# An encoder block in float32: the residual added by accumulating transfers, the token scale in the gate, and the last weight splits at set points

## The chip, the cores and the metric

The kernel runs on one core of a Trainium2 chip. The metric is the device time of one execution in microseconds (us). Engines are called as in the profile: PE (TensorE), DVE (VectorE), ACT (ScalarE), POOL (GpSimd), SP (SyncE); SP, ACT and POOL also issue DMA transfers, each from a queue of its own.

## The reference

One layer of a bidirectional encoder on a sequence of 512 tokens with 2048 features; the attention half is cut to a line.

```python
def reference(x, ...):
    h = rmsnorm(x, norm_attn)
    # input projection, two groups of attention heads, output projection, residual
    x = x + concatenate([ya, yb]) @ w_out
    h = rmsnorm(x, norm_ffn)
    x = x + (silu(h @ w_gate) * (h @ w_up)) @ w_down      # 2048 -> 5632 -> 2048
    return rmsnorm(x, norm_final)                         # y * rsqrt(mean(y*y) + eps) * gain
```

## The kernel before

**Splits.** Every product is made in near-float32 precision from three matmuls (`mm3`, L184 to L186): each operand is split into `hi`, a rounded copy that ACT casts, and `lo`, the rest, which DVE subtracts. So each piece of weight costs a DMA into a staging place (`st`, three of them), a cast on ACT and a subtraction on DVE.

**Stages.** Input projection and attention (to about 715 us), output projection (to 870), 44 units of gate and up (`unit_gu`, to 1750), and the down projection. Gate, up and most of down use a Strassen-like scheme with seven products ("11", "s3", "s2", "12", "s1", "22", "s4") of sums of weight quarters: `make` loads the four quarters (L583), adds (L593 to L603) and splits them (L612 on ACT, L613 on DVE), three products ahead of their use. `unit_gu` ends in Silu of the gate and its product with up, and `keep_combos` stores the sums and splits of the activations in `combos`.

**Down projection.** `unit_first` does the first two blocks of the inner dimension plainly and leaves the result in `acc[u, l]`, for four blocks `u` of 512 output features; each is a place of 128x1024 called `y`, `sums`, `raw` or `w` in the profile. Then come chunks 0 to 4, each with units u = 0 to 3: "(4,1)" is chunk 4, unit 1. A unit of chunks 0 to 3 has 168 matmuls of 128x256, one of chunk 4 has 126. After each product, DVE adds the bank to `acc` (`add`, L790, and L810 at the start of chunks 1 to 3); ACT copies some banks first (L806, L814). The activations' operands come by POOL's 1792 KB loads (L747), four around each start of a chunk. `unit_last` does the last four blocks plainly: 16 banks, one for each token tile t and block g, of 12 matmuls of 128x512.

**Last pieces.** `unit_last` needs eight pieces of weight of 128x1024, split by `fetch` (L119 load, L120 cast, L121 subtraction), and four tiles of activations, split by `act_tile` (L726 to L728). Before, `prepare_last` asks for the four tiles, the final gains (L896) and two pieces in unit (4,3) after its fourth product; the other six come when `unit_last` starts.

**Residual and final norm.** The activations lack the token scale `r2` (the factor of the second RMSNorm), so `add_x1` loads the residual (L843) and forms `y * r2 + x1` with two DVE operations of 128x256 (L847): for t = 0, 1 after each unit of chunk 4, for t = 2, 3 in `unit_last`. `to_rest` (L872) adds the last bank times `r2`. `finish` squares with a sum (ACT, L907), multiplies by the gain in place (DVE, L908), adds up (L910), and after the fourth block scales (L916 on ACT, L918 on DVE) and stores (L919).

**Order.** PE's instructions run in the order in which the units are written. For the other engines a list scheduler sets the order when the program is built; each engine and each DMA queue then works strictly in its order and waits on semaphores.

Of the kernel before, what the change touches and what calls it, by code (L numbers as in the profile page):

```python
# [10 lines left out]
F32 = mybir.dt.float32  # L11
F32R = mybir.dt.float32r
# [33 lines left out]
def encoder_block(ctx: ExitStack, tc: tile.TileContext, io):  # L46
# [34 lines left out]
    def w_tile():  # L81
        return work.tile([P, 512], F32, name="wk")
# [549 lines left out]
    def unit_gu(f):  # L632
        apart = f == 0
        al, be, gm = bank(), bank(), bank()
        de = bank() if apart else al
        into = {"11": al, "s3": gm, "s2": de, "12": be, "s1": de, "22": gm, "s4": de}
        first, second = slice(0, 256), slice(256, 512)
        a, b, g = w_tile(), w_tile(), w_tile()
        s1, u2, q7, c11 = a[:, first], a[:, second], b[:, first], b[:, second]
        if f % 2 == 0:  # L640
            four["raw"] = pools["mk"].tile([P, 1024], F32, name="raw").rearrange("p (a q) -> p a q", a=4)
        raw = four["raw"]
        out = (raw[:, 1], raw[:, 0]) if f % 2 == 0 else (raw[:, 2], raw[:, 3])
# [12 lines left out]
        def after(i):  # L656
            if i == 0:
                act.copy(s1, al[:, first])
            elif i == 1:
                act.copy(q7, gm[:, first])  # L660
            elif i == 2 and apart:
                dve.tensor_add(u2, de[:, first], s1)
                dve.tensor_add(q7, q7, s1)
            elif i == 2:
                act.copy(u2, al[:, first])  # L665
            elif i == 3:
                dve.tensor_add(c11, be[:, first], s1)
            elif i == 4:
                dve.tensor_add(g[:, second], de[:, first], q7)
            elif i == 5:  # L670
                dve.tensor_add(g[:, first], gm[:, first], u2)
                dve.tensor_mul(g, g, pools["rb2"])
# [45 lines left out]


    acts, acc, ops = {}, {}, {}  # L720
    nr2 = const.tile([P, NT], F32, name="nr2")

    def act_tile(f, a=None):
        if f not in acts:
# [24 lines left out]
    def unit_first():  # L749

        places_for_acc()
        load_operands(0)
        dve.tensor_scalar_mul(nr2, r2, -1.0)
        for u in range(DN):
            wh, wl = batch()
            if u == 3:
                limit[0] = len(UNITS) * 7
                make_to(NF * 7 + 2)
            b = [bank() for _ in range(NT)]
            for f in range(2):  # L760
                ws = slice(f * 512, (f + 1) * 512)
                for t in range(NT):
                    mm3(b[t], acts[f][:, t * P:(t + 1) * P], acts[f][:, 512 + t * P:512 + (t + 1) * P],
                        wh[:, ws], wl[:, ws], start=f == 0, stop=f == 1)
                yield
            for t in range(NT):
                o = acc[u, t // 2][:, (t % 2) * 512:(t % 2 + 1) * 512]
                act.copy(o[:, :256], b[t][:, :256])
                act.activation(o[:, 256:], b[t][:, 256:], AF.Copy, scale=-1.0)

    def unit_dn(c, u):
        pairs = CHUNKS[c]
# [13 lines left out]
        def flat(x):  # L786
            return x.rearrange("p (t q) -> p t q", t=2)

        def add(h, l, x):
            dve.tensor_add(r[h, l], flat(x), r[h, l])  # L790

        def product(i, some):
            n = PRODUCTS[i]
# [37 lines left out]
        for i in range(7):  # L831
            product(i, pairs[3:] if apart and i < 4 else pairs)
            after(i)
            if i0 == len(UNITS) - 1 and i == 3:
                prepare_last()
            yield
        if c == len(CHUNKS) - 1:
            for t in range(2):
                add_x1(t, u)

    def add_x1(t, u):
        x1 = w_tile()
        nc.sync.dma_start(x1, x1_kept[t, u])  # L843
        y = rest[t, u] = acc[u, t // 2][:, (t % 2) * 512:(t % 2 + 1) * 512]
        for h, r in enumerate((r2, nr2)):
            s = slice(h * 256, (h + 1) * 256)
            dve.scalar_tensor_tensor(y[:, s], y[:, s], r[:, t:t + 1], x1[:, s], op0=OP.mult, op1=OP.add)  # L847

    late = []

    def late_tile():

        n = len(late)
        if n % 3 == 0:
            late_tile.last = pools["xa"].tile([P, 7, 512], F32R, name=f"cp{(0, 1, 5, 2, 3)[n // 3]}")
        late.append(late_tile.last[:, 2 * (n % 3):2 * (n % 3) + 2].rearrange("p a q -> p (a q)"))
        return late[-1]

    def last_pair(i):
        if 2 <= i < 5:  # L860
            return wsh.tile([P, 1024], F32R, name="hi"), wsl.tile([P, 1024], F32R, name="lo")
        return late_tile(), late_tile()

    def prepare_last():
        for f in range(NF - CF, NF):
            act_tile(f, late_tile())
        load_gfin()
        fetch()
        fetch()

    def to_rest(t, g, b):
        dve.scalar_tensor_tensor(rest[t, g], b, r2[:, t:t + 1], rest[t, g], op0=OP.mult, op1=OP.add)  # L872

    def unit_last():
        w = [batch() for _ in range(8)]
        for t in range(NT):
            for g in range(4):
                b = bank()
                for f in range(CF):
                    a, (wh, wl) = acts[NF - CF + f], w[g * 2 + f // 2]  # L880
                    ws = slice((f % 2) * 512, (f % 2 + 1) * 512)
                    mm3(b, a[:, t * P:(t + 1) * P], a[:, 512 + t * P:512 + (t + 1) * P],
                        wh[:, ws], wl[:, ws], start=f == 0, stop=f == CF - 1)
                yield
                if t < 2:
                    add_x1(2 + t, g)
                to_rest(t, g, b)
                finish(t, g)

    gfin = []  # L890

    def load_gfin():
        gains = pools["mx"].tile([P, 7, 512], F32, name="w0")
        for j in range(2):
            t = gains[:, 2 * j:2 * j + 2].rearrange("p a q -> p (a q)")
# [5 lines left out]
    so_far = {}  # L901

    def finish(t, g):
        y = rest[t, g]
        jk = w_tile()
        col = ssq3[:, t * 4 + g:t * 4 + g + 1]
        act.activation(jk, y, AF.Square, accum_out=col)  # L907
        dve.tensor_mul(y, y, gfin[g // 2][:, (g % 2) * 512:(g % 2 + 1) * 512])  # L908
        v = small(1)
        dve.scalar_tensor_tensor(v, col, 1.0 / D, so_far.get(t, epsc), op0=OP.mult, op1=OP.add)  # L910
        so_far[t] = v
        if g == 3:
            r = rsqrt(v, 1)
            for c in range(4):
                if c % 2:
                    act.activation(rest[t, c], rest[t, c], AF.Copy, scale=r)  # L916
                else:
                    dve.tensor_scalar_mul(rest[t, c], rest[t, c], r)  # L918
                nc.sync.dma_start(io["out"][t * P:(t + 1) * P, c * 512:(c + 1) * 512], rest[t, c])  # L919


    side = []
# [131 lines left out]
```

## Time and profile before

| | |
|---|---|
| median of 3 runs | 2224.97 us (2224.67 to 2231.49) |
| profiled execution, own time | 2224.93 us |
| its span | 2223.2 us, granted PE clock 0.995 |
| busy: PE, DVE, ACT, POOL | 2187.6, 1661.5, 1000.2, 10.4 us |
| start of chunk 4; of `unit_last`; last matmul | 2101.48; 2160.84; 2212.49 us |

Times in the profile count from the start of the span. A row of a timeline is start, duration, engine, line, operation, output<-inputs and shape; what stands in brackets is the engine's idle time before it and who ended it. Durations of neighbours overlap a little, so the time that an operation takes in a full queue is read from start to start.

### The profile page before, as it was taken

The page shows a single profiled execution, that of the slowest core. Times are in us where ns is not written, and L with a number is a line of the kernel's source. Part 1 is how long each engine was busy: PE and PEld are TensorE (multiplying, and loading weights), DVE is VectorE, ACT ScalarE, POOL GpSimd, SP SyncE. Part 2 cuts the span into 40 slices and gives each one's busy share as a digit, 9 for nine tenths or more (in the row PEclk, how much of TensorE's full clock was granted, in tenths as well). Part 3 has the DMA queues.
Part 4 walks back from the last instruction along what each step waited for, and adds up shares of the span by engine and source line. Part 5 has one row for each costly group of instructions (what it writes and reads, how often), then busy time and mean ns, then how long its engine had stood idle before and what let it go on. Part 6 is the DMA issues. An engine that isn't in the chain of part 4 may idle for free. (4 is left out here: it accounts for less than half of the span.)

```text
span 2223.2 us, 37891 instructions
## 1 busy us (share of the span) xinstructions
PE 2187.6 (98%) x15754; PEld 2058.0 (93%) x15754; DVE 1661.5 (75%) x2373; ACT 1000.2 (45%) x1486; POOL 10.4 (0%) x23
## 2 busy tenths in 40 slices
PE   9999999999999999999999999999999999999997
PEld 8888888888888888999999999999999999999995
DVE  5655555676787447788888888888887498898897
ACT  6333333545555334444454444544444543343443
POOL 0000000000000000000000000000000000000000
PEclk9999999999999999999999999999999999999999
DMA  8222222222222453344454444544444746446344
GB/s 302 82 80 76 79 83 76 74 71 76 67 76 86 155 180 101 124 139 153 146 178 144 133 163 148 170 147 131 170 147 155 280 162 232 156 181 243 113 133 137
DMA packets 86908, 308.59 MB, mean 139 GB/s; under 512 B 10032, under 2 KB 11952, under 8 KB 84304
## 3 DMA queue, kind: packets, MB, share of 16 engines
q1 hardware_dynamic: 81696, 267.11, 36.8%
q0 software_dynamic: 2736, 34.87, 3.8%
q10 hardware_dynamic: 2304, 4.20, 0.5%
q8 instruction: 123, 2.02, 0.4%
q14 instruction: 49, 0.40, 0.1%
HBM read 261.31 MB, written 44.83 MB: 138 GB/s over the span
## 5 line engine op out<-in xcount | busy, mean ns | idle before, releaser
L612 ACT CAST hi<-m 128x1024 fp32r<-128x1024 f32 (+1 forms) x208 | 215.1, 1038 | 251.4 <-PE bank L185 124.4
L184 PE MATMUL bank<-cp,hi 128*128 128x256 f32 x1116 | 314.1, 281 | 0.1
L185 PE MATMUL bank<-cp,hi 128*128 128x256 f32 x1116 | 311.9, 280 | 0.0
L186 PE MATMUL bank<-cp,lo 128*128 128x256 f32 x1116 | 311.8, 279 | 0.0
L613 DVE TENSOR_TENSOR lo<-m,hi 128x1024 fp32r<-128x1024 f32 (+1 forms) x208 | 249.5, 1201 | 60.4 <-ACT hi L612 60.2
L121 DVE TENSOR_TENSOR lo<-st,hi 128x1024 fp32r<-128x1024 f32 (+1 forms) x136 | 165.0, 1214 | 142.6 <-ACT hi L120 138.9
L120 ACT CAST hi<-st 128x1024 fp32r<-128x1024 f32 (+1 forms) x136 | 141.7, 1042 | 194.9 <-PE bank L185 75.3
L185 PE MATMUL bank<-lo,cp 128*128 128x256 f32 (+1 forms) x738 | 209.0, 283 | 4.3 <-DVE lo L613 2.8
L184 PEld LDWEIGHTS bank<-cp,hi 128*128 128x128 f32 x1116 | 210.8, 189 | 0.5 <-ACT wk L665 0.3
L185 PEld LDWEIGHTS bank<-cp,hi 128*128 128x128 f32 x1116 | 210.3, 188 | 0.0
L186 PEld LDWEIGHTS bank<-cp,lo 128*128 128x128 f32 x1116 | 210.2, 188 | 0.0
L184 PE MATMUL bank<-hi,cp 128*128 128x256 f32 (+1 forms) x738 | 208.8, 283 | 0.7 <-DVE sums L790 0.7
L186 PE MATMUL bank<-hi,cp 128*128 128x256 f32 (+1 forms) x738 | 208.8, 283 | 0.0
L184 PE MATMUL bank<-xt,hi 128*128 128x512 f32 x512 | 206.3, 403 | 0.0
L184 PE MATMUL bank<-cp,m 128*128 128x256 f32 x732 | 205.4, 281 | 0.0
L185 PE MATMUL bank<-cp,m 128*128 128x256 f32 x732 | 204.2, 279 | 0.0
L186 PE MATMUL bank<-cp,m 128*128 128x256 f32 x732 | 204.2, 279 | 0.0
L186 PE MATMUL bank<-xt,lo 128*128 128x512 f32 x512 | 200.4, 391 | 0.0
L185 PE MATMUL bank<-xt,hi 128*128 128x512 f32 x512 | 199.9, 390 | 0.0
L612 ACT CAST m<-m 128x1024 fp32r<-128x1024 f32 (+1 forms) x112 | 116.8, 1043 | 144.2 <-PE bank L185 87.9
L613 DVE TENSOR_TENSOR m<-m,m 128x1024 fp32r<-128x1024 f32 (+1 forms) x112 | 135.3, 1208 | 39.1 <-ACT m L612 38.8
L185 PE MATMUL bank<-lo,xt 128*128 128x256 f32 x512 | 144.9, 283 | 0.7 <-DVE lo L121 0.6
(270 smaller groups left out, 5909.5 us busy)
## 6 DMA issues: line engine op xcount, KB each, us to landing
st<-w SPq DMA_DIRECT2D x199, 512.0 KB, 3.7
m<-w SPq DMA_DIRECT2D x180, 512.0 KB, 4.4
cp<-combos POOLq DMA_DIRECT2D x17, 1792.0 KB, 17.2
combos<-y SPq DMA_DIRECT2D x57, 512.0 KB, 4.5
combos<-y SPq DMA_DIRECT2D x19, 256.0 KB, 5.3
m<-w SPq DMA_DIRECT2D x12, 384.0 KB, 3.4
at<-x SPq DMA_DIRECT2D x8, 512.0 KB, 8.9
wk<-x SPq DMA_DIRECT2D x16, 256.0 KB, 5.3
```

The lines of the kernel that those rows point to most:

```text
L120: act.copy(hi[:, s], st[:, s])
L121: dve.tensor_sub(lo[:, s], st[:, s], hi[:, s].bitcast(F32))
L184: pe.matmul(out, lh, rh, start=start, stop=False, **kw)
L185: pe.matmul(out, lh, rl, start=False, stop=False, **kw)
L186: pe.matmul(out, ll, rh, start=False, stop=stop, **kw)
L612: act.copy(hi[:, :n], w[name])
L613: dve.tensor_sub(lo[:, :n], w[name], hi[:, :n].bitcast(F32))
```

## The change

The edit has six parts: the gate's factor is multiplied once more by the token scale after Silu (new L674); `unit_first` copies whole banks; the additions to `acc` are written as additions and subtractions (L790, L788); `add_x1` becomes two POOL transfers of 512 KB for each u that add the residual into `acc` in memory (L841), in chunk 2 after the second product; `prepare_last` spreads the last splits over chunks 3 and 4, with new places for them; the multiplication of the final norm writes to another place, and ACT issues half of the stores. Lines after L674 shift: L847 has gone, L872 is L875, L908 L911, L910 L913, L918 L924, L919 L922 on ACT and L925 on SP.

```diff
@@ unit_gu, after(i) @@
                 act.activation(g, g, AF.Silu, scale=-1.0)
+                dve.tensor_mul(g, g, pools["rb2"])
                 dve.tensor_mul(out[0], c11, g[:, first])
@@ unit_first @@
-                o = acc[u, t // 2][:, (t % 2) * 512:(t % 2 + 1) * 512]
-                act.copy(o[:, :256], b[t][:, :256])
-                act.activation(o[:, 256:], b[t][:, 256:], AF.Copy, scale=-1.0)
+                act.copy(acc[u, t // 2][:, (t % 2) * 512:(t % 2 + 1) * 512], b[t])
@@ unit_dn @@
         def add(h, l, x):
-            dve.tensor_add(r[h, l], flat(x), r[h, l])
+            if h == 1:
+                dve.tensor_add(r[h, l], r[h, l], flat(x))
+            else:
+                dve.tensor_sub(r[h, l], r[h, l], flat(x))
...
-            if i0 == len(UNITS) - 1 and i == 3:
-                prepare_last()
+            if c == 2 and i == 1:
+                add_x1((u + 2) % DN)
+            prepare_last(c, u, i)
             yield
-        if c == len(CHUNKS) - 1:
-            for t in range(2):
-                add_x1(t, u)
-
-    def add_x1(t, u):
-        x1 = w_tile()
-        nc.sync.dma_start(x1, x1_kept[t, u])
-        y = rest[t, u] = acc[u, t // 2][:, (t % 2) * 512:(t % 2 + 1) * 512]
-        for h, r in enumerate((r2, nr2)):
-            s = slice(h * 256, (h + 1) * 256)
-            dve.scalar_tensor_tensor(y[:, s], y[:, s], r[:, t:t + 1], x1[:, s], op0=OP.mult, op1=OP.add)
+
+    def add_x1(u):
+        for l in range(2):
+            pool.dma_start(acc[u, l].rearrange("p (t q) -> p t q", t=2),
+                           x1_kept[2 * l:2 * l + 2, u].rearrange("t p q -> p t q"), accum_op=OP.add)
...
-    def prepare_last():
-        for f in range(NF - CF, NF):
-            act_tile(f, late_tile())
-        load_gfin()
-        fetch()
-        fetch()
+    def prepare_last(c, u, i):
+        if (c, u, i) in ((3, 3, 3), (4, 1, 1), (4, 1, 4), (4, 3, 3), (4, 3, 4)):
+            fetch()
+        if (c, u, i) == (4, 2, 4):
+            load_gfin()
+        if c == 4 and u == 0 and i in (1, 4):
+            for f in range(2):
+                act_tile(NF - CF + f + (i == 4) * 2, take())
 
     def to_rest(t, g, b):
-        dve.scalar_tensor_tensor(rest[t, g], b, r2[:, t:t + 1], rest[t, g], op0=OP.mult, op1=OP.add)
+        y = rest[t, g] = acc[g, t // 2][:, (t % 2) * 512:(t % 2 + 1) * 512]
+        dve.tensor_add(y, b, y)
@@ unit_last @@
-                if t < 2:
-                    add_x1(2 + t, g)
                 to_rest(t, g, b)
                 finish(t, g)
@@ finish @@
         act.activation(jk, y, AF.Square, accum_out=col)
-        dve.tensor_mul(y, y, gfin[g // 2][:, (g % 2) * 512:(g % 2 + 1) * 512])
+        z = done_y[t, g] = rest[t - 1, g] if t else spare[g] if g < 3 else w_tile()
+        dve.tensor_mul(z, y, gfin[g // 2][:, (g % 2) * 512:(g % 2 + 1) * 512])
...
                 if c % 2:
-                    act.activation(rest[t, c], rest[t, c], AF.Copy, scale=r)
+                    act.activation(z, z, AF.Copy, scale=r)
+                    act.dma_start(o, z)
                 else:
-                    dve.tensor_scalar_mul(rest[t, c], rest[t, c], r)
-                nc.sync.dma_start(io["out"][t * P:(t + 1) * P, c * 512:(c + 1) * 512], rest[t, c])
+                    dve.tensor_scalar_mul(z, z, r)
+                    nc.sync.dma_start(o, z)
```

The scheduler gives the engines the following orders. First SP's queue around chunk 4, before: the quarters of units (4,1) to (4,3) (L583, `m` and `st`), the residual's loads (L843), the activation tiles (L726) and the last pieces of weight (L119).

```order
382 L896 DMA w_22754<-gfin 128x1024 x2
383 L583 DMA m_22270<-w 128x768
384 L583 DMA st<-w 128x768
385 L843 DMA wk<-x_kept 128x512 x2
386 L583 DMA m_22268<-w 128x768
387 L583 DMA m_22264<-w 128x768
388 L583 DMA m_22459<-w 128x768
389 L583 DMA st<-w 128x768
390 L843 DMA wk<-x_kept 128x512 x2
...
394 L726 DMA st<-acts_kept 128x512 x3
...
397 L119 DMA st<-w 128x1024 x2
...
399 L119 DMA st<-w 128x1024 x6
```

The same queue after:

```order
378 L119 DMA st<-w 128x1024
...
383 L726 DMA st<-acts_kept 128x512
...
385 L726 DMA st<-acts_kept 128x512
386 L583 DMA m_22320<-w 128x768
387 L726 DMA st<-acts_kept 128x512 x2
388 L583 DMA m_22318<-w 128x768
389 L583 DMA m_22314<-w 128x768
390 L583 DMA st<-w 128x768
391 L119 DMA st<-w 128x1024 x2
392 L583 DMA m_22508<-w 128x768
...
395 L583 DMA st<-w 128x768
396 L119 DMA st<-w 128x1024 x5
```

The activation tiles and three of the eight pieces now stand among the quarters of chunk 4, and the residual's loads are gone. DVE's queue between units (4,2) and (4,3), before, with the residual's operations (L847):

```order
2097 L790 TENSOR_TENSOR raw<-wk,raw 128x2x256
2098 L613 TENSOR_TENSOR m_22532<-m_22264,m_22531 128x768
2099 L790 TENSOR_TENSOR raw<-bank,raw 128x2x256
2100 L613 TENSOR_TENSOR lo<-m_22453,hi 128x768
2101 L790 TENSOR_TENSOR raw<-wk,raw 128x2x256
2102 L790 TENSOR_TENSOR w_18264<-bank,w_18264 128x2x256
2103 L596 TENSOR_TENSOR st<-st,m_22457 128x768
2104 L613 TENSOR_TENSOR lo<-st,hi 128x768
2105 L790 TENSOR_TENSOR raw<-bank,raw 128x2x256
2106 L598 TENSOR_TENSOR m_22453<-st,m_22453 128x768
2107 L847 SCALAR_TENSOR_TENSOR raw<-raw,r_99,wk 128x256
2108 L790 TENSOR_TENSOR w_18264<-bank,w_18264 128x2x256
```

And after; the last row is the `lo` of product s2 of unit (4,3):

```order
2144 L790 TENSOR_TENSOR w_18307<-w_18307,bank 128x2x256
2145 L613 TENSOR_TENSOR lo<-st,hi 128x768
2146 L790 TENSOR_TENSOR raw<-raw,bank 128x2x256
2147 L596 TENSOR_TENSOR st<-st,m_22508 128x768
2148 L121 TENSOR_TENSOR m_22784<-st,m_22783 128x1024
2149 L598 TENSOR_TENSOR m_22504<-st,m_22504 128x768
2150 L788 TENSOR_TENSOR w_18307<-w_18307,bank 128x2x256
2151 L613 TENSOR_TENSOR m_22689<-m_22510,m_22688 128x768
2152 L121 TENSOR_TENSOR m_22809<-st,cp_22445 128x1024
2153 L613 TENSOR_TENSOR lo<-m_22504,hi 128x768
```

Two subtractions L121 for `unit_last` now stand among the additions and splits of chunk 4; two more (2116 and 2125) stand further ahead. POOL's queue around chunk 2, after; before, it has only the L747:

```order
16 L747 DMA cp_19616<-combos 128x3584
17 L841 DMA raw<-x_kept 128x2x512
18 L841 DMA w_18307<-x_kept 128x2x512
19 L747 DMA cp_20287<-combos 128x3584
20 L747 DMA cp_20517<-combos 128x3584
21 L747 DMA w_20519<-combos 128x3584
22 L747 DMA cp_20521<-combos 128x3584
23 L841 DMA w_18307<-x_kept 128x2x512 x2
24 L841 DMA y<-x_kept 128x2x512 x3
25 L841 DMA sums<-x_kept 128x2x512
```

Two accumulating transfers stand ahead of the loads at the start of chunk 2, and six behind them.

More of the change, by code (lines that the diff above doesn't have):

```diff
@@ L720, in encoder_block @@
     acts, acc, ops = {}, {}, {}
-    nr2 = const.tile([P, NT], F32, name="nr2")
     def act_tile(f, a=None):
@@ L752, in unit_first @@
         load_operands(0)
-        dve.tensor_scalar_mul(nr2, r2, -1.0)
         for u in range(DN):
@@ L849, in encoder_block @@
[L849 to L857, printed above, removed]
-    def last_pair(i):
-        if 2 <= i < 5:
-            return wsh.tile([P, 1024], F32R, name="hi"), wsl.tile([P, 1024], F32R, name="lo")
-        return late_tile(), late_tile()
-    def prepare_last():
-        for f in range(NF - CF, NF):
-            act_tile(f, late_tile())
-        load_gfin()
-        fetch()
-        fetch()
+    def add_x1(u):
+        for l in range(2):
+            pool.dma_start(acc[u, l].rearrange("p (t q) -> p t q", t=2),
+                           x1_kept[2 * l:2 * l + 2, u].rearrange("t p q -> p t q"), accum_op=OP.add)
@@ new lines, in encoder_block, with take @@
+    free, left, spare, gains = [], [0, 1, 5], [], []
+    def last_pair(i):
+        if i == 0:
+            return place(7, F32R), place(9, F32R)
+        if i < 3:
+            return take(), take()
+        if i == 3:
+            return place(at[0] % 6, F32R), place((at[0] + 1) % 6, F32R)
+        if i == 4:
+            return take(), place((at[0] + 2) % 6, F32R)
+        return wsh.tile([P, 1024], F32R, name="hi"), wsl.tile([P, 1024], F32R, name="lo")
+    def take():
+        if not free:
+            w = pools["xa"].tile([P, 7, 512], F32R, name=f"cp{left.pop(0)}")
+            free.extend(w[:, 2 * j:2 * j + 2].rearrange("p a q -> p (a q)") for j in range(3))
+        return free.pop(0)
@@ L892, in load_gfin @@
     def load_gfin():
-        gains = pools["mx"].tile([P, 7, 512], F32, name="w0")
+        gains.append(pools["mx"].tile([P, 7, 512], F32, name="w0"))
+        spare.extend(gains[0][:, j] for j in range(4, 7))
         for j in range(2):
-            t = gains[:, 2 * j:2 * j + 2].rearrange("p a q -> p (a q)")
+            t = gains[0][:, 2 * j:2 * j + 2].rearrange("p a q -> p (a q)")
             nc.sync.dma_start(t, io["gfin"][:, j * 1024:(j + 1) * 1024].to_broadcast([P, 1024]))
@@ L899, in encoder_block @@
     ssq3 = const.tile([P, 16], F32, name="ssq3")
-    so_far = {}
+    so_far, done_y = {}, {}
     def finish(t, g):
@@ L914, in finish @@
             for c in range(4):
+                z = done_y[t, c]
+                o = io["out"][t * P:(t + 1) * P, c * 512:(c + 1) * 512]
                 if c % 2:
-                    act.activation(rest[t, c], rest[t, c], AF.Copy, scale=r)
-                else:
-                    dve.tensor_scalar_mul(rest[t, c], rest[t, c], r)
-                nc.sync.dma_start(io["out"][t * P:(t + 1) * P, c * 512:(c + 1) * 512], rest[t, c])
+                    act.activation(z, z, AF.Copy, scale=r)
+                    act.dma_start(o, z)
+                else:
+                    dve.tensor_scalar_mul(z, z, r)
+                    nc.sync.dma_start(o, z)
     side = []
```

## The prediction

> **What bounds the kernel now.** I read the page's first part, then busy time by stages, then the chain of PE's waits, then the timelines of the stages in which PE waits.
>
> The first row is the span; the second says that PE is busy for 98% of it, so only places where PE stops can give time back.
>
> ```profile
> span 2223.2 us, 37891 instructions
> PE 2187.6 (98%) x15754; PEld 2058.0 (93%) x15754; DVE 1661.5 (75%) x2373; ACT 1000.2 (45%) x1486; POOL 10.4 (0%) x23
> ```
>
> Busy time by stage: the first row lies in the gate-and-up stage, the second is the middle of the down projection (chunk 2), the third 46 us of chunk 4, the last the 16 banks of `unit_last`.
>
> ```profile
> core 0: us, PE busy (x) PEld busy (x) DVE busy (x) ACT busy (x) POOL busy (x), PEclk, DMA share, GB/s
> 1000.00:1600.00 600.00, 599.95 (x5054) 599.44 (x5053) 509.59 (x616) 290.20 (x390) 0.00 (x0) 1.00 0.47 153
> 1947.00:2028.00 81.00, 78.15 (x671) 77.98 (x671) 69.98 (x75) 32.15 (x36) 2.11 (x4) 0.98 0.53 194
> 2104.42:2150.35 45.93, 45.93 (x392) 45.93 (x391) 45.81 (x67) 21.52 (x29) 0.00 (x0) 1.00 0.37 116
> 2160.84:2212.89 52.05, 46.82 (x194) 35.34 (x192) 43.56 (x107) 21.57 (x43) 0.00 (x0) 1.00 0.47 157
> ```
>
> Gate-and-up: PE never waits, DVE is at 85%. Chunk 4: PE never waits, but DVE has 0.12 us to spare in 46. `unit_last`: PE loses over 5 us even by this count. PE's waits from 1770 us on (engine, line, releaser: total, times, longest):
>
> ```profile
> PE bank L184 <- DVE wk L810: 8.5, 3, 2.8
> PE bank L185 <- DVE cp L121: 3.1, 4, 0.8
> PE bank L185 <- DVE lo L613: 2.8, 1, 2.8
> PE bank L185 <- DVE lo L121: 1.4, 2, 1.3
> ```
>
> L810 and L613 are the starts of chunks 1 to 3 and of chunk 0. The L121 rows are `unit_last`, waiting for the splits of its own weights. How much that stage loses in all (first and last matmul, and three between; 192 matmuls):
>
> ```profile
> 2160.84 0.40 PE L184 MATMUL bank<-cp,cp 128*128 128x512 f32 x1
> ...
> 2167.38 0.50 PE L185 MATMUL bank<-lo,cp 128*128 128x512 f32 x1 [1.29 <-DVE lo L121]
> ...
> 2178.35 0.50 PE L185 MATMUL bank<-cp,cp 128*128 128x512 f32 x1 [0.76 <-DVE cp L121]
> 2178.69 0.40 PE L186 MATMUL bank<-cp,cp 128*128 128x512 f32 x1
> ...
> 2212.49 0.39 PE L186 MATMUL bank<-cp,cp 128*128 128x512 f32 x1
> ```
>
> From 2178.69 to 2212.49 lie 147 steps without a wait, 0.230 us each. The 44 steps before them take 17.85 us instead of 44 x 0.230 = 10.12: `unit_last` loses 7.7 us, all in its first 18.
>
> **The change, part by part.**
>
> (1) *Set points for the last splits.* Gain: if every half that `unit_last` needs early is there, the 7.7 us go but for about 0.1 at its first matmul: -7.6. In the new order only three L121 stand between DVE's last chunk-4 additions and the first L872, and their pieces are the last three of eight, used 5 us or more later at 0.230 us a matmul. I take -7.6; if half of the waits return, -3.8.
>
> Cost: the splits go into chunk 4, where DVE is full. I count DVE's queue between two fixed points. It starts with the addition of `wk` in unit (4,0), which waits for ACT's copy L806 of the bank that PE has just closed, so DVE cannot be ahead there:
>
> ```profile
> 2104.42 0.69 DVE L790 TENSOR_TENSOR y<-wk,y 128x512 f32<-128x512 f32 x1 [0.70 <-ACT wk L806]
> ...
> 2132.24 0.95 DVE L613 TENSOR_TENSOR m<-m,m 128x768 fp32r<-128x768 f32 x1
> 2133.10 0.48 DVE L847 SCALAR_TENSOR_TENSOR y<-y,r,wk 128x256 f32<-128x256 f32 x1
> 2133.50 0.48 DVE L847 SCALAR_TENSOR_TENSOR y<-y,nr,wk 128x256 f32<-128x256 f32 x1
> ...
> 2136.50 0.69 DVE L790 TENSOR_TENSOR w<-bank,w 128x512 f32<-128x512 f32 x1
> 2137.10 0.95 DVE L613 TENSOR_TENSOR lo<-m,hi 128x768 fp32r<-128x768 f32 x1
> ...
> 2166.10 2.36 DVE L121 TENSOR_TENSOR lo<-st,hi 128x1024 fp32r<-128x1024 f32 x2
> 2168.38 0.48 DVE L847 SCALAR_TENSOR_TENSOR y<-y,r,wk 128x256 f32<-128x256 f32 x1
> ```
>
> From start to start: 0.866 for a 128x768 operation, 0.40 for an L847, 0.60 for a 128x512 one, 1.14 for an L121 (2.28 for two). It ends with the `lo` of product s2 of unit (4,3), which PE needs at 2150.3 (chunk 4 starts at 2101.5; three units of 126 matmuls at 0.1177 us, two products of 18). Before, 67 operations stand there: 31 x 0.866 + 24 x 0.60 + 12 x 0.40 = 46.0 us, which is the 45.93 of the window, so the count is sound. After, the 12 L847 are gone and one 128x768, three L728 and four L121 have come: 32 x 0.866 + 24 x 0.60 + 3 x 0.60 + 4 x 1.14 = 48.5 us. DVE is at that `lo` 2.6 us late without a single wait of its own, and PE stops for that long.
>
> DVE will also wait. Each split stands behind its load and ACT's cast, in one queue with the additions and the `lo` that PE needs. What these take (the first row is a load's landing around chunk 4; the second the cast, as it was in `unit_last`):
>
> ```profile
> st<-w SPq DMA_DIRECT2D x5, 512.0 KB, 4.2
> 2162.10 1.05 ACT L120 CAST cp<-st 128x1024 fp32r<-128x1024 f32 x1 [2.23 <-DMA st<-w]
> ```
>
> Walking SP's, ACT's and DVE's new queues with these durations, I get PE waits of about 0.2 us at s2 of (4,1), 1.2 at s4 of (4,1), where a fetch's cast stands ahead of L612 on ACT, and 1.1 each at s2 of (4,2) and of (4,3), where fetches wait for one of the three `st` places: 3.6 to 3.8 in all. A landing 1 us later at two of these places, as the 2.23 us idle above shows that ACT does wait for them, makes it 5.8. Ends: +2.6 and +6; I take +3.8, nearest to the walk.
>
> (2) *add_x1 as accumulating DMAs.* Removed: 32 L847, of which the 12 above are in the count of (1); the rest stood in `unit_last` beside the waits and are in the 7.7. Their 16 loads leave SP's queue, four 256 KB loads of `acts_kept` come earlier. Added: 8 POOL transfers of 512 KB. No accumulating transfer is in the trace; the nearest rows:
>
> ```profile
> st<-w SPq DMA_DIRECT2D x199, 512.0 KB, 3.7
> cp<-combos POOLq DMA_DIRECT2D x17, 1792.0 KB, 17.2
> 1934.54 0.53 POOL L747 DMA_DIRECT2D cp<-combos  x1 [80.52 <-PE bank L186]
> ...
> 1937.19 0.54 POOL L747 DMA_DIRECT2D cp<-combos  x1 [0.59 <-issue]
> ```
>
> So 3.7 to 17.2 us each. The first two are queued ahead of the four loads of 1934.5 and wait only for unit (1,2)'s last addition, one unit (168 x 0.1177 = 19.8 us) before that, so they end in time; the next two are issued at about 1938 into the burst of these loads (2 x 0.5 MB on 7.3). Each is needed two units, 40 us, after the place where it is issued. Cost 0; were (2)'s 1 MB in the burst to hold up weights by their share of it, 17.2 x 1/7.3 = 2.4 us. I take 0.
>
> (3) *Gate factor.* 44 more 128x512 multiplications, as L672:
>
> ```profile
> L613 DVE TENSOR_TENSOR lo<-m,hi 128x1024 fp32r<-128x1024 f32 x91 | 111.1, 1221 | 35.9 <-ACT hi L612 35.8
> L672 DVE TENSOR_TENSOR wk<-wk,rb 128x512 f32<-128x512 f32 x30 | 20.5, 683 | 0.0
> ```
>
> That is 0.60 from start to start, 44 x 0.60 = 26 us of DVE in a stage of 880, 85% to 88%. The cover is the first row: DVE waits 35.8 us in 30 units for ACT's casts, having run ahead of PE by as much as the buffers let it; 0.6 of 1.2 us per unit goes. Worked out over the stage, every `lo` is written at least 6 us before PE takes it. Cost 0; if the cover were gone, 26 us.
>
> (4) *unit_first's copies, additions turned round.* 32 half copies become 16; the wait there is a load's. The operation at the chunks' starts (L810, 3 x 2.8 us) keeps its place and its wait. 0, at most -0.4.
>
> (5) *Final norm.* After the last matmul:
>
> ```profile
> 2212.92 0.75 DVE L872 SCALAR_TENSOR_TENSOR w<-bank,r,w 128x512 f32<-128x512 f32 x1 [0.23 <-PE bank L186]
> 2213.76 0.63 ACT L907 ACTIVATE wk<-w 128x512 f32<-128x512 f32 x1 [1.87 <-DVE w L872]
> ...
> 2214.51 0.69 DVE L908 TENSOR_TENSOR w<-w,w 128x512 f32<-128x512 f32 x1 [0.85 <-ACT wk L907]
> 2215.12 0.15 DVE L910 SCALAR_TENSOR_TENSOR sm<-ssq,sm 128x1 f32<-128x1 f32 x1
> ...
> 2217.72 0.71 ACT L916 ACTIVATE w<-w,sm 128x512 f32<-128x512 f32 x1
> 2218.03 0.38 SPq L919 DMA_DIRECT2D out<-sums  x1
> 2218.51 0.90 SPq L919 DMA_DIRECT2D out<-w  x2
> ```
>
> L908 waits for the Square because both use one place. With a place of its own it runs beside it, and L910 can follow the Square at 2214.5 instead of 2215.12: -0.55 to -0.6. Two of the four last transfers are issued by ACT; SP's last pair takes 0.90 in a row, so about -0.2 at the end, or 0 if ACT's issue delays its second scaling by as much. I take -0.7. The Trainium skill ("DMA: Bandwidth & Descriptors", Rules for kernel authors) says that spreading transfers over the issuing queues brings no bandwidth and only saves the sequencer's issue time. By that rule alone this part is -0.2 and no more; the row agrees, since 0.90 for two is issue.
>
> **Sum.** The profiled execution took 2224.93 us (span 2223.2 and 1.7 around it), 0.04 under the median of 2224.97. -7.6 + 3.8 + 0 + 0 - 0.7 = -4.5, so 2220.4; I add 0.4, because in (1) one late landing costs 1 us and an early one wins nothing: 2220.8.
>
> **The rivals.**
>
> *Chunk 4 hides its splits.* Then 2224.9 - 7.6 - 0.7 = 2216.6. For it: chunk 2's row has DVE at 86%, so work may be pulled ahead of chunk 4. Against it: the new order already has one split there, and the count starts at an addition that PE's pace holds back.
>
> *The stall only moves.* Chunk 4's landings are late by 2 us each, five fetches and four activation tiles behind three `st` places, and PE loses 7 there: 2224.9 - 7.6 + 7 - 0.7 = 2223.6, and up to 2225.5 if 2 us of waits stay in `unit_last`. For it: DVE has no spare time to catch up.
>
> *Slower: the accumulating transfers hold the queue.* Place: start of chunk 2. POOL's queue has the first two ahead of the load of chunk 2's fourth pair, which PE needs after four early products, 4 x 18 x 0.1177 = 8.5 us after 1934.5. They have the 20 us from unit (1,2)'s end. If they take over 14 us each and loads wait for them, PE waits for the rest. [...] It makes the kernel slower by the bound below from 15.5 us each on (2 x 15.5 - 20 = 11). Against it: the 1792 KB load takes 17.2 us, four of them together, and 512 KB 3.7. [...]
>
> **Chances.** About 0.3% (6.7 us) is what a measurement of this kernel can tell from no change: faster is under 2218.3, slower over 2231.6. The forecast (DVE late in chunk 4, 2218 to 2223) 0.70; hidden 0.14; moved 0.10; slower 0.06. Faster: all of the hidden case and a little of the forecast, 0.16. Same: 0.78. The range is 2216.6 (hidden) to 2225.5 (moved), which leaves out the slower rival and a few hundredths at each end.
>
> **What would show it.** Right: no PE wait on L121 after the start of `unit_last`, about 44 us from its first to its last matmul; in chunk 4 PE waits of 3 to 5 us, released by DVE's `lo` L613 or additions, with L121 or ACT's L120 just ahead of them; gate-and-up without PE waits and DVE at 88%; the three L810 waits unchanged; the Square and the multiplication side by side. Wrong: PE waits on `cp<-combos` or weights in chunks 2 and 3, a POOL issue far above 0.53, waits in gate-and-up, or chunk 4 without waits.

## The result, and the profile after

The changed kernel takes 2242.97 us (median of 4 runs, 2242.88 to 2248.13), the kernel before beside it 2225.23 us: ratio 1.008, 95% interval 1.0064 to 1.0096. It is slower, by some 18 us (0.8%), where 2220.8 us and no change that a measurement can tell were forecast. Here and below, a ratio is estimated from all runs of both kernels, so it can differ by up to 0.1% from the quotient of the medians.

The page of the changed kernel begins:

```profile
span 2241.3 us, 37925 instructions
PE 2202.1 (98%) x15754; PEld 2071.1 (92%) x15754; DVE 1680.4 (75%) x2384; ACT 999.0 (45%) x1470; POOL 20.1 (1%) x31
```

PE has as many instructions as before and is busy 14.5 us longer, so part of the loss is not in waits at all. The stages, each measured from its first to its last matmul in the two timelines (differences in us, span against span):

| stage | before | after | difference |
|---|---|---|---|
| until gate-and-up begins | 863.2 | 862.7 | -0.5 |
| gate-and-up | 887.4 | 902.3 | +14.9 |
| `unit_first` | 21.9 | 21.9 | 0 |
| chunks 0 to 4 | 388.3 | 400.0 | +11.7 |
| `unit_last` | 51.7 | 44.4 | -7.3 |
| after the last matmul starts | 10.7 | 10.0 | -0.7 |
| sum | 2223.2 | 2241.3 | +18.1 |

The last part of the program does what the prediction said. Busy time in `unit_last` (PE is the first pair of numbers), and the tail:

```profile
2186.96:2231.70 44.74, 44.74 (x194) 35.91 (x192) 31.10 (x81) 15.83 (x37) 0.00 (x0) 1.00 0.21 71
```

```profile
2231.76 0.69 DVE L875 TENSOR_TENSOR w<-bank,w 128x512 f32<-128x512 f32 x1 [1.17 <-PE bank L186]
2232.48 0.63 ACT L909 ACTIVATE wk<-w 128x512 f32<-128x512 f32 x1 [2.08 <-DVE w L875]
2232.48 0.69 DVE L911 TENSOR_TENSOR w<-w,w 128x512 f32<-128x512 f32 x1
...
2233.24 0.16 DVE L913 SCALAR_TENSOR_TENSOR sm<-ssq,sm 128x1 f32<-128x1 f32 x1
...
2236.58 0.34 ACTq L922 DMA_DIRECT2D out<-w  x1
```

PE never stops in `unit_last`; the Square and the multiplication start at the same time, and the sum follows them. PE's waits in chunk 4:

```profile
PE bank L184 <- DVE sums L790: 1.5, 1, 1.5
PE bank L185 <- DVE lo L613: 0.9, 2, 0.5
PE bank L185 <- DVE m L613: 0.6, 1, 0.6
```

With the restart after each, these stops take 4.1 us. The longest stands at product s4 of (4,1); ahead of it ACT waits with a last piece's cast for its load, and the cast L612 that the chunk needs stands behind:

```profile
2147.97 1.05 ACT L120 CAST cp<-st 128x1024 fp32r<-128x1024 f32 x1 [2.69 <-DMA st<-w]
2148.93 1.57 ACT L612 CAST hi<-m 128x768 fp32r<-128x768 f32 x2
```

Two places where nothing was expected show new things: gate-and-up, and chunk 2. In gate-and-up, a stretch of 600 us held 5054 matmuls before; now:

```profile
1000.00:1600.00 600.00, 596.61 (x4962) 594.42 (x4962) 518.59 (x633) 284.74 (x382) 0.00 (x0) 1.00 0.45 150
```

PE is idle for 3.4 us, but 92 matmuls are missing, which is 11 us: the matmuls themselves are slower, at a granted clock of 1.00 in both. From start to start, leaving out stops, a step takes 0.1197 us instead of 0.1186. Over 44 x 168 = 7392 steps that is 8.2 us of the stage's 14.9. The rest is waits, the named ones all of one kind:

```profile
PE bank L184 <- DVE wk L669: 3.3, 6, 1.7
```

The longest of them, in the timelines of ACT, DVE and PE:

```profile
1534.15 0.62 ACT L626 CAST y<-sums 128x512 fp32r<-128x512 f32 x1 [3.41 <-DMA combos<-y]
1534.67 1.04 ACT L612 CAST hi<-st 128x1024 fp32r<-128x1024 f32 x1
```

```profile
1534.80 0.69 DVE L627 TENSOR_TENSOR y<-sums,y 128x512 fp32r<-128x512 f32 x1 [3.07 <-ACT y L626]
...
1536.88 1.21 DVE L613 TENSOR_TENSOR lo<-st,hi 128x1024 fp32r<-128x1024 f32 x1
1538.13 1.23 DVE L593 TENSOR_TENSOR st<-m,st 128x1024 f32<-128x1024 f32 x1
1539.27 0.41 DVE L669 TENSOR_TENSOR wk<-bank,wk 128x256 f32<-128x256 f32 x1
```

```profile
1539.74 0.39 PE L184 MATMUL bank<-cp,m 128*128 128x256 f32 x1 [1.66 <-DVE wk L669]
```

Read upward: PE's product s4 adds to the bank in which s1 stands, and may not begin before DVE has read it (L669). L669 stands in DVE's queue behind splits, these behind ACT's casts, and ACT stands 3.4 us at L626, the fourth split of `keep_combos`, because its place `y` is one of three and the first store from them has not landed.

The kernel before has this wait too (2.2 us on average, in each of the 19 units in which `keep_combos` makes its splits), but there it does not reach PE. The same unit before:

```profile
1520.92 0.62 ACT L626 CAST y<-sums 128x512 fp32r<-128x512 f32 x1 [2.16 <-DMA combos<-y]
1527.66 0.42 DVE L669 TENSOR_TENSOR wk<-bank,wk 128x256 f32<-128x256 f32 x1
1528.70 0.28 PE L184 MATMUL bank<-cp,m 128*128 128x256 f32 x1
```

L669 ends at 1528.08 and s4 begins at 1528.70, without a wait: 0.62 us to spare. Over the 19 units the margin was 0.5 to 0.9 us. The new multiplication takes 0.60 us of the same queue, and in the changed kernel L669 ends after PE has come to s4 in 15 of the 19 units, by up to 1.8 us.

In the chunks, PE's step went from 0.11646 to 0.11783 us (0.00137 x 3192 = 4.4 us), chunk 4 adds 4.1 us of stops, and unit (2,1) has two new ones, of 2.0 and 1.1 us (one of 0.9 us in unit (1,1) has gone):

```profile
1985.10 0.38 PE L185 MATMUL bank<-lo,cp 128*128 128x256 f32 x1 [1.84 <-DVE lo L613]
1997.52 0.36 PE L184 MATMUL bank<-hi,cp 128*128 128x256 f32 x1 [0.88 <-DVE sums L790]
```

Ahead of the first, DVE waits for a weight (the second row is its load on SP's queue):

```profile
1982.09 1.23 DVE L593 TENSOR_TENSOR st<-m,st 128x1024 f32<-128x1024 f32 x1 [5.44 <-DMA m<-w]
1970.28 0.33 SPq L583 DMA_DIRECT2D m<-w  x1
```

This weight was asked for at 1970.3 and landed 11.7 us later, where the median of such loads is 4.4 us. POOL's queue shows what was under way: the four loads of 1792 KB, and an accumulating transfer behind them.

```profile
1934.46 1.25 POOL L841 DMA_DIRECT2D raw<-x_kept  x1 [62.58 <-DVE raw L790]
1940.49 1.20 POOL L841 DMA_DIRECT2D w<-x_kept  x1 [4.79 <-issue]
1952.80 1.25 POOL L747 DMA_DIRECT2D cp<-combos  x2 [11.11 <-PE bank L186]
...
1960.93 1.22 POOL L841 DMA_DIRECT2D w<-x_kept  x1 [5.17 <-issue]
```

The transfer of 1960.9 landed after 21.2 us; the other seven, outside the burst, after 5.6 to 9.4 us. Start and landing show one thing more: each accumulating transfer that stands next behind another in POOL's queue was issued 0.3 us after that one had landed, so the queue stood still that long. Why it waits is not shown. The first two took 15.4 us in this way, and the loads were issued 2.9 us after the second had landed.

### The profile page after: what moved, and what is told of

The parts are those of the page before. It is cut to its first block, busy times and chain, and to the rows that moved or that the text cites. A ratio compares the mean times of both kernels' runs of the same rounds, so it can differ in the third digit from the quotient of the medians.

```text
span 2241.3 us, 37925 instructions
## 1 busy us (share of the span) xinstructions
PE 2202.1 (98%) x15754; PEld 2071.1 (92%) x15754; DVE 1680.4 (75%) x2384; ACT 999.0 (45%) x1470; POOL 20.1 (1%) x31
## 5 line engine op out<-in xcount | busy, mean ns | idle before, releaser
L612 ACT CAST hi<-m 128x1024 fp32r<-128x1024 f32 (+1 forms) x208 | 214.4, 1036 | 254.6 <-PE bank L185 98.2
L185 PE MATMUL bank<-cp,hi 128*128 128x256 f32 x1116 | 316.3, 283 | 0.0
L121 DVE TENSOR_TENSOR lo<-st,hi 128x1024 fp32r<-128x1024 f32 (+1 forms) x136 | 165.1, 1214 | 142.4 <-ACT hi L120 141.6
L185 PE MATMUL bank<-lo,cp 128*128 128x256 f32 (+1 forms) x738 | 210.7, 285 | 5.7 <-DVE lo L613 5.7
L185 PEld LDWEIGHTS bank<-cp,hi 128*128 128x128 f32 x1116 | 210.2, 188 | 0.0
L185 PE MATMUL bank<-cp,m 128*128 128x256 f32 x732 | 207.1, 283 | 0.0
L185 PE MATMUL bank<-xt,hi 128*128 128x512 f32 x512 | 200.0, 391 | 0.0
L612 ACT CAST m<-m 128x1024 fp32r<-128x1024 f32 (+1 forms) x112 | 116.6, 1041 | 148.4 <-PE bank L185 66.2
L185 PEld LDWEIGHTS bank<-lo,cp 128*128 128x128 f32 x738 | 139.7, 189 | 7.6 <-DVE lo L613 6.5
```

Of the source, the lines that this page charges most:

```text
L121: dve.tensor_sub(lo[:, s], st[:, s], hi[:, s].bitcast(F32))
L185: pe.matmul(out, lh, rl, start=False, stop=False, **kw)
L612: act.copy(hi[:, :n], w[name])
```

## The experiments

In the rows of c1, c_late, c2 and c3, L748, L791, L807 and L844 are the changed kernel's L747, L790, L806 and L841.

The first theory on the slower matmuls (A): the change took away a tile of 16 bytes a partition (`nr2`, which occupies 32), and all places on that side of the memory, the split weights, staging places and `m` and `w` places, moved down by 32 bytes; the operands `cp` on the other side did not. The rival (B): the busier DVE of gate-and-up disturbs them.

**a_pad: the old places under the changed kernel.**

```diff
-    r2 = const.tile([P, NT], F32, name="r2")
+    r2 = const.tile([P, 4 * NT], F32, name="r2")[:, :NT]
```

> The changed kernel with one constant tile made larger (r2 64 bytes a partition instead of 32), so that the split weights, the staging places and the w places stand again where they stood before the change (the removal of nr2 had moved them down by 32 bytes). No instruction differs. Theory A (the 32 bytes set the pace of the matmuls): the step from matmul to matmul in gate-and-up goes back from 0.1197 to 0.1186 us, in chunk 0 from 0.117 to 0.114, in chunk 2 from 0.118 to 0.113; 8 + 2 + 3 = 13 us less, about 2230 us. Theory B (the pace follows the busier DVE of gate-and-up, places do not matter): nothing moves, 2243 us.

Measured: 2235.64 us against 2228.12 (1.0034, 1.0021 to 1.0046). The step in gate-and-up is 0.1186 us again: A. In the chunks hardly any of it came back (0.1176; chunks 0 and 2 stayed at 0.118 and 0.117, where A had 0.114 and 0.113), so A does not explain their pace. PE's waits on L669 did not shrink; they come in nearly every second unit:

```profile
PE bank L184 <- DVE wk L669: 5.1, 14, 0.9
```

**b_nopad: the new places under the kernel before.**

```diff
-    r2 = const.tile([P, NT], F32, name="r2")
+    r2 = const.tile([P, 2 * NT], F32, name="r2")
...
-    nr2 = const.tile([P, NT], F32, name="nr2")
+    nr2, r2 = r2[:, NT:], r2[:, :NT]
```

> The kernel before with r2 and nr2 in one constant tile, so that the places of split weights, staging and w move down by the same 32 bytes as in the change. No instruction differs otherwise. Theory A (the 32 bytes set the pace): 13 us more, about 2238 us, with 0.1197 us a step in gate-and-up. Theory B (DVE's load sets it): 2225 us as before.

Measured: 2236.64 us against 2228.12 (1.0031, 1.0018 to 1.0043), so a move of 32 bytes with no other edit costs some 8 us. Gate-and-up:

```profile
1000.00:1600.00 600.00, 600.00 (x5011) 599.87 (x5010) 505.73 (x610) 286.06 (x387) 0.00 (x0) 1.00 0.46 150
```

PE is never idle and does 43 matmuls fewer than before in the same time. B is out: DVE's work is that of the kernel before.

**a_nomul: without the gate's second multiplication.**

```diff
                 act.activation(g, g, AF.Silu, scale=-1.0)
-                dve.tensor_mul(g, g, pools["rb2"])
```

> The changed kernel without the second multiplication of the gate by the token scale (44 DVE operations of 128x512; the activations then lack the scale, which is left out of the result). Places as in the changed kernel. Theory A: the pace stays at 0.1197 us a step, but PE's waits on L669 in gate-and-up (some 5 us) go: about 2238 us. Theory B: pace and waits go back: about 2228 us.

Measured: 2238.95 us against 2228.12 (1.0042, 1.0028 to 1.0056). The step stays at 0.1197 us, the waits on L669 are gone, gate-and-up takes 895.6 us instead of 902.3. So the multiplication, which was priced at nothing, costs 6.7 us there.

```profile
1000.00:1600.00 600.00, 599.46 (x5006) 599.19 (x5006) 504.81 (x608) 285.44 (x385) 0.00 (x0) 1.00 0.46 151
```

**a_noacc: without the accumulating transfers.**

```diff
-            if c == 2 and i == 1:
-                add_x1((u + 2) % DN)
```

> The changed kernel without the eight accumulating transfers (the residual is left out of the result). If these transfers make the weight late for which PE waits 1.8 us in unit (2,0) or (2,1), that wait goes and the time is about 2241 us; if they cost nothing, 2243 us; if they cost more elsewhere, less than 2240. The pace of the matmuls stays in both theories.

Measured: 2242.23 us against 2228.12 (1.0055, 1.0034 to 1.0075). The stop of 2.0 us at the weight in chunk 2 is gone and the chunks take 397.0 us instead of 400.0, but the whole is only 0.7 us under the changed kernel's 2242.97 and 3.4 under its second median (a_again, below). By itself it settles little.

**b_pad32 and b_pad64: the kernel before moved up by 32 and by 64 bytes** (`[P, 4 * NT]` and `[P, 6 * NT]` in r2's line).

> The kernel before with its places moved up by 32 bytes (down by 32 is b_nopad). If the pace depends on the address modulo 64 bytes, the step in gate-and-up is 0.1197 us as in b_nopad, and the time 8 to 10 us above before. If it depends on a distance or a boundary in another way, it may be 0.1186 or another value.

> The kernel before with its places moved up by 64 bytes. Modulo 64 bytes nothing changes: 0.1186 us a step and the time of before, if that is the rule; if any move changes the pace, another value. The down projection's chunks 0 and 2 (0.114 us a step in the trace of before, 0.118 in all others so far) show whether that pace belongs to the places or differs from execution to execution.

Measured: 2225.84 us (0.9995, 0.9986 to 1.0004) and 2248.39 us (1.0091, 1.0075 to 1.0108), both against 2227.56. A rule modulo 64 bytes is refuted in both directions: 32 bytes up, the step in gate-and-up is 0.1181 us; 64 bytes up, 0.1200, and all five chunks run at 0.1200 too. That is the slowest kernel of the study, and it differs from the kernel before in the size of one unused piece of memory:

```profile
1000.00:1600.00 600.00, 599.81 (x4995) 599.25 (x4994) 503.50 (x606) 285.05 (x385) 0.00 (x0) 1.00 0.46 150
```

**b_both: both sides moved by 32 bytes.**

```diff
+    side_const = enter("side_const", 1, side="right")
     work = enter("work", 4, side="right")
...
-    ones = const.tile([P, 1], F32, name="ones")
+    ones = side_const.tile([P, 1], F32, name="ones")
```

> The kernel before with all places of both sides of the memory moved down by 32 bytes (one constant went from the left side to the right end), so that the distance between the split weights and the activations' operands stays as before and only absolute addresses move. If the pace goes by distance, 0.1186 us a step and the time of before; if by the absolute place of the left side, 0.1197 and 8 us more, as b_nopad.

Measured: 2230.05 us against 2226.92 (1.0005, 0.9991 to 1.0018). The left side stands where it stands in b_nopad, the pace is that of before:

```profile
1000.00:1600.00 600.00, 599.92 (x5053) 599.39 (x5052) 510.18 (x617) 291.35 (x393) 0.00 (x0) 1.00 0.46 153
```

So it is the distance between the two sides that counts, not the address of either. The pattern of long and short steps within a product is the same, to 0.0005 us, in before, a_pad and b_both, and another one in after, b_nopad and a_nomul. It is not only the distance within one matmul: of the eight pairs of a product, the last two (`w0`, `w1`) take both operands from the side that moved, and the step behind the first matmul of the last pair still went from 0.1135 to 0.1200 us. In one table (step in gate-and-up, by how far the weights' places stand from those of before, relative to `cp`):

| -32 bytes (after, b_nopad, a_nomul, a_noacc) | 0 (before, a_pad, b_both) | +32 (b_pad32) | +64 (b_pad64) |
|---|---|---|---|
| 0.1197 us | 0.1186 | 0.1181 | 0.1200 |

**a_y1: another place for one of the four splits**, on top of a_pad.

```diff
-            y = y_tile(F32R).rearrange("p (n q) -> p n q", n=2)[:, :n]
+            y = y_tile(F32R) if n == 2 else w_tile().bitcast(F32R)
+            y = y.rearrange("p (n q) -> p n q", n=n)
```

> The changed kernel with its old places (r2's tile enlarged, as in a_pad) and with another staging place (a work tile) for the one split in keep_combos that is half as wide, so that its four splits no longer share three places y. If PE's waits on L669 in gate-and-up come from ACT standing in its queue for the store that frees y (3.4 us idle before L626), they go: 8.8 us of stops in a_pad to under 1, about 2228 us against 2235.6. If they come from DVE's share alone (one operation more per unit), they stay: 2235.

Measured: 2225.86 us against 2227.56 (0.9993, 0.9983 to 1.0004), 9.8 us less than a_pad (9.2 when each is taken against the kernel before beside it). Gate-and-up takes 886.5 us instead of 896.9, with the multiplication in it and DVE at 89%:

```profile
1000.00:1600.00 600.00, 600.00 (x5061) 600.00 (x5060) 531.72 (x648) 290.53 (x393) 0.00 (x0) 1.00 0.46 153
```

DVE's share was never the bound; the shared place was.

**c1: a_y1 with the accumulating transfers at other points.**

```diff
-            if c == 2 and i == 1:
-                add_x1((u + 2) % DN)
+            if (c, u, i) in PLACES_X1:
+                add_x1(PLACES_X1[c, u, i])
...
+    PLACES_X1 = {(2, 2, 1): 0, (2, 2, 5): 1, (2, 3, 3): 2, (3, 1, 5): 3}
```

> As a_y1, and the eight accumulating transfers issued outside the bursts of loads at the chunks' starts (after products of units (2,2), (2,3) and (3,1)). If the transfers in the burst make weights late, DVE's longest wait for m<-w at chunk 2's start (5.4 us) falls to 3 and PE loses 2 us less than in a_y1: about 2226 us. If the burst is slow by itself, no difference from a_y1.

Measured: 2223.9 us against 2227.56 (0.9983, 0.997 to 0.9996). The stops left chunk 2 and came back, as 2.2 and 1.1 us, at the start of chunk 3. The intervals of c1 and a_y1 overlap, so this run left the question open; c3 takes it up.

**a_again: the changed kernel once more.**

> The changed kernel once more, unchanged, beside the others on their chip. If its excess over the kernel before belongs to the kernel, it is again some 15 to 18 us (about 2243 against 2227), with 0.1197 us a step in gate-and-up and 5 to 9 us of stops there; if the first comparison was the chip's, less.

Measured: 2245.59 us against 2226.92 (1.0076, 1.0058 to 1.0094): the loss belongs to the kernel.

**c_late: c1 with the set points undone.**

```diff
-        if (c, u, i) in ((3, 3, 3), (4, 1, 1), (4, 1, 4), (4, 3, 3), (4, 3, 4)):
-            fetch()
-        if (c, u, i) == (4, 2, 4):
-            load_gfin()
-        if c == 4 and u == 0 and i in (1, 4):
-            for f in range(2):
-                act_tile(NF - CF + f + (i == 4) * 2, take())
+        if (c, u, i) == (4, 3, 3):
+            for f in range(CF):
+                act_tile(NF - CF + f, take())
+            load_gfin()
+            fetch()
+            fetch()
```

> c1 with the set points undone: the four activation tiles, the gains and two pieces are asked for in unit (4,3) after its fourth product, the other six by unit_last, as in the kernel before. If the set points move DVE's lateness from unit_last to chunk 4, chunk 4's stops (about 4.4 us) vanish, unit_last takes 51 instead of 44.2 us, and the time is some 3 us above c1: 2227. If the chunk-4 stops have another cause, they stay and the time is 7 us above c1.

Measured: 2221.4 us against 2226.92 (0.9974, 0.9963 to 0.9985). PE's waits from chunk 4 to the end, in c1 and then in c_late:

```profile
PE bank L184 <- DVE sums L791: 1.6, 1, 1.6
PE bank L185 <- DVE lo L613: 0.9, 2, 0.5
PE bank L185 <- DVE m L613: 0.6, 1, 0.6
PE bank L184 <- ACT wk L807: 0.3, 1, 0.3
```

```profile
PE bank L185 <- DVE lo L121: 0.7, 1, 0.7
PE bank L184 <- DVE w L791: 0.2, 1, 0.2
```

Chunk 4's stops (4.4 us in c1) are gone, as expected. `unit_last` was expected back at 51 us and takes 45.2, only 1.0 more than in c1. So the set points are not what freed `unit_last`: they gain 1.0 us there and cost 4.4 in chunk 4. What did free it is argued, not shown. c_late keeps the change's other parts: the L847 and the residual's loads are gone, and the last pieces have the new places. SP's queue points at the loads. Before, it issued the first last piece 6.2 us ahead of the stage, behind two loads of the residual; in c_late, 11.1 us ahead of it (2166.57), all eight in a row (the first two rows are before, the third c_late):

```profile
2151.45 0.90 SPq L843 DMA_DIRECT2D wk<-x_kept  x2
2154.62 2.40 SPq L119 DMA_DIRECT2D st<-w  x2
2155.43 15.56 SPq L119 DMA_DIRECT2D st<-w  x8
```

**c2: c1 with chunk 4's four L121 on POOL** (`pool.tensor_sub` in `fetch` for the four pieces asked for in chunk 4).

> c1 with the subtractions of the four pieces that are split in chunk 4 on POOL instead of DVE (4 x 1.14 us less on DVE between the fixed points, which is more than the 2.6 us by which its queue was too long). If DVE's queue is the cause of chunk 4's stops, they fall from about 4.4 to 1 to 2 us: about 2221 us. If POOL's subtraction is slow or disturbs DVE, they stay or grow: 2224 or more.

Measured: 2226.77 us against 2226.92 (0.9994, 0.9983 to 1.0005), with 4.8 us of stops in chunk 4: no gain. POOL's subtractions, and DVE's operations in the same 46 us:

```profile
2129.90 2.41 POOL L121 TENSOR_TENSOR cp<-st,cp 128x1024 fp32r<-128x1024 f32 x1 [78.21 <-ACT cp L120]
2136.68 3.08 POOL L121 TENSOR_TENSOR cp<-st,cp 128x1024 fp32r<-128x1024 f32 x1 [4.37 <-ACT cp L120]
```

```profile
L596 DVE TENSOR_TENSOR st<-st,m 128x768 f32<-128x768 f32 x3 | 4.5, 1491 | 0.0
L593 DVE TENSOR_TENSOR st<-m,st 128x768 f32<-128x768 f32 x3 | 4.4, 1476 | 0.0
```

In c1 these take 956 and 955 ns. The means hide what happens. Each of POOL's four subtractions held up one DVE operation, to 2.5 to 3.0 us instead of 0.95, and it ended 0.8 us after POOL's; the addition of a bank just before this one, while POOL ran, took its usual 0.67:

```profile
2137.45 0.67 DVE L791 TENSOR_TENSOR sums<-sums,bank 128x512 f32<-128x512 f32 x1
2138.05 2.53 DVE L593 TENSOR_TENSOR st<-m,st 128x768 f32<-128x768 f32 x1
```

That is some 6.9 us lost on DVE against 4.6 saved. The Trainium skill ("GPSIMD Engine Reference", Key points) says that GpSimd shares its SBUF interfaces with VectorE and that they contend when the DVE instruction has two SBUF inputs. All four that were held up have two, the addition of the bank has one, and the trace agrees.

**c3: c_late with the accumulating transfers behind the last burst** (after products of units (3,2), (3,3), (4,0) and (4,1)).

> c_late with all eight accumulating transfers behind the last burst of loads (after products of units (3,2), (3,3), (4,0) and (4,1)). In c1 and c_late one of them still fell into the burst at chunk 3's start (issued 2028.0, burst from 2019.2), and PE lost 2.2 and 1.1 us there, where it had lost them in chunk 2 before. If a transfer in the burst is the cause, both stops go and DVE's waits for m<-w fall from 5.6 to 3 us: about 3 us less than c_late, 2218 to 2219 against some 2227. If the stops belong to the place of chunk 3 or to the burst itself, they stay: 2221.

Measured: 2216.91 us against 2225.93 (0.9962, 0.9948 to 0.9975). DVE's waits for weights at the chunks' starts, in c_late and then in c3:

```profile
DVE st L593 <- DMA m<-w: 7.0, 4, 5.6
```

```profile
DVE st L593 <- DMA m<-w: 4.5, 2, 2.9
```

Both stops at chunk 3's start are gone. Issued from 2043.7 on, the same eight transfers stop PE nowhere in chunk 3:

```profile
2019.98 0.53 POOL L748 DMA_DIRECT2D cp<-combos  x1 [0.24 <-issue]
2043.72 1.24 POOL L844 DMA_DIRECT2D y<-x_kept  x1 [23.21 <-DVE y L791]
2049.52 1.20 POOL L844 DMA_DIRECT2D y<-x_kept  x1 [4.57 <-ACT hi L612]
```

c3 is faster than the kernel before by 0.4%, and so than the changed kernel: it is the changed kernel with the old places, one split's place elsewhere, the transfers behind the last burst, and without the set points.

## Why the prediction was wrong

The step that failed is the gate factor's "cost 0", together with a term that is missing, the places. Both stand in gate-and-up, which took 14.9 us more where 0 was forecast; that it might wait there was on the prediction's own list of signs. Behind the missing term stands its first reading, that with PE busy 98% of the time only places where PE stops can give time back: a PE that never stops can still go slower.

- **Splits at set points, gain -7.6:** the size came out (-7.3), the cause named for it did not, so the agreement is luck. c_late shows that the set points are worth 1.0 of it; the rest came with the other parts of the change.
- **Splits at set points, cost +3.8:** right, with its mechanism. Forecast were 0.2, 1.2, 1.1 and 1.1 us at s2 and s4 of (4,1) and s2 of (4,2) and (4,3); the timeline has 0.5, 1.7, 0.9 and 1.1, together 4.1. c_late shows that they belong to the set points.
- **`unit_first` and the additions, 0; final norm, -0.7:** right (21.9 us in both kernels, L810 8.5 and 8.6; -0.7, as the two operations side by side).
- **Accumulating transfers, 0:** wrong, by 2 to 3 us. The prediction had the price, the burst's share of 2.4 us, and took 0. a_noacc (the chunks 3.0 us shorter) and c3 show that a transfer in the burst makes weights late. The slower rival, that POOL's queue holds up the loads, did not happen, as PE waited for no `cp<-combos`; but the first two transfers, one after the other, left only 2.9 us before these loads.
- **Gate factor, 0:** failed, by 6.7 us (a_nomul). The cover was checked where DVE writes for PE (`lo`, 6 us ahead), not where PE waits for DVE to read: L669 must empty a bank within one product after it is filled. There 0.5 to 0.9 us were to spare, behind ACT's wait for a store, and the multiplication takes 0.60. a_y1 removes the wait and keeps the multiplication, and PE's waits are gone.
- **What had no term:** the places. The removal of `nr2` belongs to the edit and was not priced. It is worth +8.2 us in gate-and-up (a_pad, b_nopad). How much of the 4.4 us by which the chunks' pace slowed belongs to it stays open: b_nopad has 3.6 us more in the chunks than before, but a_pad, with the old places, got only 0.8 back.

By the profiles, 8.2, 6.7, 4.4 and 3.0 us come to 22.3 us, of 22.2 between 2220.8 and 2242.97.

## What to carry to other kernels

When work is added to an engine with spare time, check every wait on that engine's queue in both directions, also where the bound engine waits for a bank to be read, and who shares the places that its queue neighbours need. A transfer of 0.5 MB cost nothing or 2 to 3 us here, depending on whether it falls into a burst of others, so its place is worth a row of the timeline. Where the matrix engine is busy all the time, count its instructions in a fixed stretch: that shows a slower pace, which no wait shows.

## What the runs showed of the hardware

- The step from matmul to matmul (128x256, at a granted clock of 1.00) depends on how far the two sides of the memory from which it takes its operands are apart: 0.1181 to 0.1200 us in gate-and-up for moves of 32 and 64 bytes. Inside one setting it differs from operand to operand: in the changed kernel, the L185 matmuls take 0.1230 us with `cp0`, `cp2` and `cp4` and 0.1170 with `cp1`, `cp3` and `cp5`. The mechanism stays open; so does the best distance, of which four values were tried.
- Chunks 0 and 2 have a pace that differs between programs with the same places: 0.1133 or 0.1178 us in units 1 to 3 of chunk 0 (a_y1, c1), and the changed kernel itself had 0.1173 and 0.1187 there in two executions. Of the eight traces with the distance of before, seven have 0.1133 in one of these chunks or both (a_pad in neither); of the seven at other distances, none has. What else sets it was not found.
- An accumulating transfer of 512 KB takes POOL 1.2 us to issue, a plain load of 1792 KB 0.53. It landed after 5.5 to 11.5 us outside a burst (after, c1, c3) and after 21 us in one (after, c1). The next accumulating transfer in POOL's queue was never issued before the one ahead of it had landed; where nothing else was awaited, it followed by 0.3 us.
- While POOL subtracts 128x1024 with both inputs in SBUF (2.4 to 3.1 us), a DVE operation with two SBUF inputs that starts after it ends 0.8 us after it, 2.5 to 3.0 us from its own start instead of 0.95 (c2). One with an input from a bank takes its usual time.
